# Keeping the seven x operands of six matrix products in DRAM after the first product, and GpSimd out of these products

## Chip, cores and metric

One NeuronCore of a Trainium2 chip runs the whole kernel. The metric is device time in microseconds (us) of one execution, as the median of several runs. The engines are named as the profile names them: PE (TensorE matmul), PEld (TensorE weight load), DVE (VectorE), ACT (ScalarE), POOL (GpSimd) and SP (SyncE, which here issues every DMA).

## What is computed

One layer of a hybrid encoder, for 2048 prompt tokens and 64 sample tokens (2112 rows), model width 1024, all in float32:

```
xn = rms_norm(x)                    # 2112 x 1024
xa, za, q, k, v, zb, ga, gb = split(xn @ w_in)      # eight blocks of 1024 columns
ya = rglru(conv(xa)) * silu(za)
yb = diff_attn(rms(q), rms(k), v) * silu(zb)
y  = x + (sigmoid(ga) * (ya @ w_proj_a) + sigmoid(gb) * (yb @ w_proj_b)) @ w_out
```

The case is about the products of `xn` with the six column blocks q, k, v, zb, ga and gb. They are run as six groups of 1024 x 1024 weights: v, then half of q with half of k, zb, the other halves of q and k, ga, gb.

## The kernel before

The kernel has four stages in time. The first makes xn, the products for xa and za and the recurrence ("Hawk" stage, 0 to about 490 us), and writes xn to the DRAM tile `xn_d`. The second, `Stage "a"` (490 to 1650 us), runs the six groups above. The third is the attention (to about 2554 us). The fourth, `Stage "d"`, runs three more groups with the same code: ya @ w_proj_a, yb @ w_proj_b and the output projection.

A group multiplies 2112 x 1024 by 1024 x 1024. It does one level of a Strassen-Winograd scheme: token tiles i and i + 8 (128 tokens each) and the two halves of the inner and of the output dimension are the 2 x 2 blocks of one **item**, and an item needs seven products in place of eight. The seven operands of x are the blocks A11, A12, A22 and the sums S1, S2, S3, S4; those of the weights are B11, T1, T2, B21, T3, B22, T4. Every operand is a float32 tile of 128 x 512 (x) or 128 x 2048 (w), and is split in a high and a low part (`hi` by a cast to fp32r on ACT, `lo` as the rest), since a float32 product is made of three fp32r matmuls (hi*hi, hi*lo, lo*hi: lines 63, 64 and 65 of `mm3`). With four blocks of 128 along the inner half, one product is 12 matmuls of 512 columns. This is a **slot**. `ITEMS` gives the order: items 0 and 1 take turns (14 slots), then items 2 and 3 alone (7 slots each), the 64 sample tokens "s" (5 slots, `sample`), items 4 and 5 alone, items 6 and 7 in turns: 61 slots in a group.

The order of the work is written by hand: `at(s, fn)` puts `fn` on the list of slot s, and `tick()` issues the list behind the product of that slot, weights (`plan_w`) ahead of x (`plan_x`). PE, DVE, ACT and POOL issue in exactly this order; the order of SP's queue is set by the framework's scheduler. Each engine works its queue in order, and an instruction that waits holds all behind it.

`plan_x` (line 162) for an item whose first slot is b: at b - 9 and b - 8 four loads of 256 KB from `xn_d` into raw tiles (`load`, line 169); at b - 6 to b - 4 the four sums (`add`, line 173: S1 and S2 on DVE, S3 and S4 on POOL); then for the operand of slot k at k - 4 its `hi` (line 178, ACT) and at k - 3 its `lo` (line 181: A11, S1, S3, S4 on POOL, the other three on DVE). Operands lie in `xo`, five buffers of two parts each, which a slot's products release.

`plan_w` (line 118) loads a group's weights (line 129) from b - 13 on, where b is the group's first slot, makes T1 to T4 (line 135, DVE) at b - 7, b - 5 and b - 1, and cuts the seven operands in high and low parts from b - 6 to b + 6. An operand is cut in two halves of 128 x 1024: two casts on ACT (line 143), then the low part of one half on DVE and of the other on POOL (line 145).

Results leave PSUM by ACT copies and DVE adds in `pair` (lines 222 to 247). In the q and k groups `out_qk` then squares (774), reduces (775), takes a root (787, 788, newton 55 to 57) and scales (797) every half on ACT and DVE; `turn_qk` transposes it on PE (812) into one of two PSUM buffers, and ACT, DVE (828 for q) and POOL (823, the low part of k) make its parts, of which two (q) or three (k) are stored, 256 KB each, in rows of 512 bytes (816). The other groups store a half once, after an ACT sigmoid for the gates (747, stored in 749), and after a DVE product too for zb (752, 753).

Of the kernel before, what the change touches and what calls it, by code (L numbers as in the profile page):

```python
# [11 lines left out]
F32 = mybir.dt.float32  # L12
# [7 lines left out]
P = 128  # L20
# [57 lines left out]
class Stage:  # L78
    def __init__(self, nc, tc, c, name, ident, order, bufs, first=()):
        self.nc, self.ident = nc, ident  # L80
        self.tc, self.c, self.first = tc, c, first
        pool = lambda n, b, **kw: c.enter_context(tc.tile_pool(name=n + name, bufs=b, reuse_waits=RW, **kw))
        place = lambda i: pool(f"wq{i}_", 1, side="right")
        self.wq = [place(i) for i in range(7)]
        self.xr = pool("xr", 2, side="right")
        self.xo = pool("xo", 5, side="right")
        self.wq += [place(i) for i in range(7, 15)]
        self.wfree = list(order)
        self.bufs = bufs
        self.sb = pool("sb", 1)  # L90
        self.wk = pool("wk", 1) if name == "a" else None
        self.pm = pool("pm", 4, space=PSUM)
        self.pz = pool("pz", 2, space=PSUM)
        self.pt = pool("pt", 2, space=PSUM)
        self.now = -99
        self.tasks = {}

    def at(self, s, fn):
        self.tasks.setdefault(max(s, self.now), []).append(fn)
# [23 lines left out]
    def plan_w(self, src, ws, b, pick):  # L123
        nc, q, at = self.nc, {}, self.at

        def load(nm, i):
            q[nm] = self.wtile(pick=pick)
            for k in range(0, 4, 2):
                nc.sync.dma_start(q[nm][1][:, k : k + 2, :], src[i, :, k : k + 2, :])

        def sub(dst, x, y, over=None):
            q[dst] = q[over] if over else self.wtile(pick=pick)
            for i in range(2):
                s = slice(2 * i, 2 * i + 2)
                nc.vector.tensor_tensor(q[dst][1][:, s, :], q[x][1][:, s, :], q[y][1][:, s, :], op=ALU.subtract)  # L135

        def cut(nm):
            at_, raw = q[nm]
            soon = pick if pick is None else nm in ("B11", "T1")
            (hi_at, hi), (lo_at, lo) = self.wtile(F32R, soon), self.wtile(F32R, soon)  # L140
            for i in range(2):
                s = slice(2 * i, 2 * i + 2)
                nc.scalar.copy(hi[:, s, :], raw[:, s, :])  # L143
                eng = nc.vector if i == 0 else nc.gpsimd
                eng.tensor_tensor(lo[:, s, :], raw[:, s, :], hi.bitcast(F32)[:, s, :], op=ALU.subtract)  # L145
            ws[nm] = hi, lo, (hi_at, lo_at)
            if nm != "T2":
                self.wfree.append(at_)

        at(b - 13, lambda: (load("B11", 0), load("B12", 1)))  # L150
        at(b - 8, lambda: load("B22", 3))
        at(b - 7, lambda: sub("T1", "B12", "B11"))
        at(b - 6, lambda: cut("B11"))
        at(b - 5, lambda: sub("T2", "B22", "T1"))
        at(b - 4, lambda: (load("B21", 2), cut("T1")))
        at(b - 2, lambda: cut("T2"))
        at(b - 1, lambda: (sub("T3", "B22", "B12", "B12"), sub("T4", "B21", "T2", "T2")))
        for i, nm in enumerate(("B21", "T3", "B22", "T4")):
            at(b + 2 * i, lambda nm=nm: cut(nm))


    def plan_x(self, src, item, xs, s, b):
        nc, q, at = self.nc, {}, self.at
        V, G = nc.vector, nc.gpsimd

        def load(nm, t, half):
            tn = TOK[t][1]
            q[nm] = self.raw(nm)
            nc.sync.dma_start(q[nm][:, :, :tn], src[t, :, half * 4 : half * 4 + 4, :tn])

        def add(eng, dst, x, y, op, over=None):
            q[dst] = q[over] if over else self.raw(dst)
            eng.tensor_tensor(q[dst], q[x], q[y], op=op)

        def hi(nm):
            o = self.xo.tile([P, 2, 4, P], F32R, name="x8")
            xs[nm] = o[:, 0], o[:, 1]
            nc.scalar.copy(xs[nm][0], q[nm])  # L178

        def lo(nm, eng):  # L180
            eng.tensor_tensor(xs[nm][1], q[nm], xs[nm][0].bitcast(F32), op=ALU.subtract)  # L181

        if item == "s":
            def both():
                o = self.xo.tile([P, 2, 4, P], F32R, name="x8")
                for i in range(2):
                    r = q[f"A{i}"][:, :, :TS]
                    xs[f"A{i}"] = o[:, i]
                    nc.scalar.copy(o[:, i, :, :TS], r)
                    V.tensor_tensor(o[:, i, :, TS:], r, o.bitcast(F32)[:, i, :, :TS], op=ALU.subtract)  # L190

            at(b - 5, lambda: (load("A0", NT - 1, 0), load("A1", NT - 1, 1)))
            at(b - 2, both)
            return
        u, v = item, item + 8
        at(b - 9, lambda: (load("A21", v, 0), load("A22", v, 1)))
        at(b - 8, lambda: (load("A11", u, 0), load("A12", u, 1)))
        at(b - 6, lambda: add(V, "S1", "A21", "A22", ALU.add))
        at(b - 5, lambda: (add(V, "S2", "S1", "A11", ALU.subtract), add(G, "S3", "A11", "A21", ALU.subtract, "A21")))
        at(b - 4, lambda: add(G, "S4", "A12", "S2", ALU.subtract))  # L200
        off = b - s[0]
        for nm, k, eng in zip(("A11", "S1", "S2", "A12", "S3", "S4", "A22"), s, (G, G, V, V, G, G, V)):
            at(k + off - 4, lambda nm=nm: hi(nm))
            at(k + off - 3, lambda nm=nm, eng=eng: lo(nm, eng))

# [77 lines left out]
        self.tick()  # L283


    def run(self, groups):
        plan, b = [], 0
        for g, (wsrc, xsrc, out) in enumerate(groups):
            ws = {}
            last = g == len(groups) - 1 and self.first  # L290
            self.plan_w(wsrc, ws, b, False if last else None)
            for its in ITEMS:
                n = len(its)
                gens = []
                for k, it in enumerate(its):
                    xs = {}
                    s = [b + i for i in range(5)] if it == "s" else [b + n * i + k for i in range(7)]
                    self.plan_x(xsrc, it, xs, s, s[0] - 1 if it == 4 else s[0])
                    gens.append((it, xs, ws, out, s))
                plan.append((gens, b))  # L300
                b += 5 if its == "s" else 7 * n
        self.now = -20
        while self.now < 0:
            self.tick() if self.now in self.tasks else self.skip()
        E = mybir.EngineType
        self.c.enter_context(self.tc.manual_schedule(engines={E.PE, E.DVE, E.Activation, E.Pool}))
        for items, b in plan:
            assert self.now == b
            gens = []
            for it, xs, ws, out, s in items:  # L310
                done = out(it, s)
                if it == "s":
                    self.sample(xs, ws, done)
                else:
                    gens.append(self.pair(it, xs, ws, done))
            for _ in range(7 if gens else 0):
                for g in gens:
                    next(g)
                    self.tick()
        while self.tasks:  # L320
            self.tick() if self.now in self.tasks else self.skip()
# [6 lines left out]
def stream_step_kernel(ctx, tc, I, O):  # L328
# [9 lines left out]
    m1_d = dram.tile([NT, P, D], F32, name="m1_d")  # L338
    strip_d = dram.tile([NH, P * STRIP], F32, name="strip_d")
    xn_d = dram.tile([NT, P, KT, P], F32, name="xn_d")  # L340
    ya_d = dram.tile([NT, P, KT, P], F32, name="ya_d")
    yb_d = dram.tile([NT, P, KT, P], F32, name="yb_d")
    mt_d = dram.tile([NT, P, KT, P], F32, name="mt_d")
# [382 lines left out]
    with ExitStack() as c:  # L726
# [81 lines left out]
        def turn_qk(h0, isk, t, c):  # L808
# [10 lines left out]
            if isk:  # L819
                kf, lo = new(), new()  # L820
                nc.scalar.mul(kf, pq, gk)
                nc.scalar.copy(hi.bitcast(F32R), kf)
                nc.gpsimd.tensor_tensor(lo.bitcast(F32R), kf, hi, op=ALU.subtract)
                put(kT_d, kf)
            else:
                nc.scalar.mul(hi.bitcast(F32R), pq, gq)
                lo = new()
                nc.vector.scalar_tensor_tensor(lo.bitcast(F32R), pq, gq, hi, op0=ALU.mult, op1=ALU.subtract)
# [3 lines left out]
        def strips():  # L832
# [25 lines left out]
            (I["wg"][2], xn_d, out_qk(4)),  # L858
            (I["wg"][4], xn_d, out_gate(ga_d, False)),
            (I["wg"][5], xn_d, out_gate(gb_d, False)),  # L860
        ])

    with ExitStack() as c:
        c.enter_context(tc.manual_schedule(engines={mybir.EngineType.PE}))
# [353 lines left out]
        def take(name):  # L1218
            slot = [9e9]
            rings[name][1].append(slot)  # L1220
            return slot
# [331 lines left out]
```

## Time and profile before

| | us |
|---|---|
| median of 3 runs (lowest to highest) | 3129.71 (3129.59 to 3131.15) |
| the profiled execution | 3132.76 |
| its span, first to last instruction | 3131.0 |
| PE busy in the span | 2854.5 (91%) |
| DVE busy | 2070.2 (66%) |
| ACT busy | 1703.7 (54%) |
| POOL busy | 1447.7 (46%) |
| DMA, share of 16 engines | 42.3%, 406.18 MB |

Busy time of PE counts matmuls that overlap, so it does not show how near PE is to its best; the distance from one matmul's start to the next does. A granted clock of 1.0 is TensorE's upper level, 0.5 its lower one.

### The profile page before, as it was taken

The numbers are of one execution on the slowest core, as the hardware profiler recorded it, in microseconds if no ns is written. First come the engines' busy times: TensorE is split into PE (matmuls) and PEld (weight loads), VectorE is DVE, ScalarE is ACT, GpSimd is POOL, SyncE is SP. The second block draws the span as 40 slices with busy tenths as digits, with TensorE's granted clock in tenths as the row PEclk, the third lists the DMA queues.
The fourth block names the chain that finished last, engine by engine and source line by source line (L and its number), as shares of the span: only waits on it lengthen the run. The fifth ranks groups of instructions, "written<-read, shape, count | busy, mean of one in ns | idle before, by whom it ended". The sixth has DMA issues, their size and how long they took to land.

```text
span 3131.0 us, 43652 instructions
## 1 busy us (share of the span) xinstructions
PE 2854.5 (91%) x14808; PEld 2392.7 (76%) x14808; DVE 2070.2 (66%) x4147; ACT 1703.7 (54%) x3251; POOL 1447.7 (46%) x900
## 2 busy tenths in 40 slices
PE   6999996999979989699997998998999979979899
PEld 6888885777758777587785987887888768868677
DVE  7776786267685776735525677777777775475764
ACT  7776774345544455545445766676676653333432
POOL 0000005355454544545544655555465457786743
PEclk9999998999989999899998999999999989989999
DMA  4121232335534346354346453544543434545553
GB/s 139 60 75 53 70 122 84 124 128 149 181 100 156 129 131 184 108 165 138 107 117 170 124 141 112 144 127 122 135 117 116 128 101 148 196 149 196 177 172 129
DMA packets 356671, 408.96 MB, mean 131 GB/s; under 512 B 48448, under 2 KB 242400, under 8 KB 356448
## 3 DMA queue, kind: packets, MB, share of 16 engines
q1 hardware_dynamic: 356448, 406.18, 42.3%
q8 instruction: 117, 1.92, 0.3%
q14 instruction: 106, 0.87, 0.1%
HBM read 272.22 MB, written 131.37 MB: 129 GB/s over the span
## 4 chain that ended last, share of the span: by engine, by line
PE 45%; DVE 11%; ACT 4%; issue 2%; POOL 2%; DMA 1%; SPq 0%; DVEq 0%; POOLq 0%; ACTq 0%
PE acc L65 7%; PE acc L63 7%; PE acc L64 7%; PE accv L1008 5%; PE pk L942 3%; PE pk L943 3%; PE ptt L1000 3%; PE accv L1131 2%; PE acz L65 1%; PE acz L63 1%; PE acz L64 1%; DVE o L1172 1%; DVE S L955 1%; ACT S L973 1%; DVE w L135 1%
## 5 line engine op out<-in xcount | busy, mean ns | idle before, releaser
L65 PE MATMUL acc<-w,x 128*128 128x512 f32 x1728 | 694.9, 402 | 82.8 <-POOL x L181 55.4
L63 PE MATMUL acc<-w,x 128*128 128x512 f32 x1728 | 699.0, 405 | 14.8 <-ACT sc L230 7.7
L64 PE MATMUL acc<-w,x 128*128 128x512 f32 x1728 | 689.0, 399 | 11.2 <-DVE w L145 10.8
L65 PEld LDWEIGHTS acc<-w,x 128*128 128x128 f32 x1728 | 334.8, 194 | 168.6 <-POOL x L181 64.1
L145 POOL TENSOR_TENSOR w<-w,w 128x1024 fp32r<-128x1024 f32 x63 | 180.1, 2860 | 574.7 <-ACT w L143 549.4
L63 PEld LDWEIGHTS acc<-w,x 128*128 128x128 f32 x1728 | 335.7, 194 | 87.1 <-ACT sc L230 8.5
L64 PEld LDWEIGHTS acc<-w,x 128*128 128x128 f32 x1728 | 335.2, 194 | 81.8 <-DVE w L145 11.8
L181 POOL TENSOR_TENSOR x<-xA,x 128x512 fp32r<-128x512 f32 x144 | 217.3, 1509 | 311.9 <-ACT x L178 298.2
L942 PE MATMUL pk<-k,Q 128*128 128x512 f32 (+2 forms) x640 | 263.2, 413 | 48.8 <-DVE S L955 17.7
L955 DVE TENSOR_SCALAR_CACHE_REDUCE S<-pk,far 128x1024 f32<-128x1024 f32 x224 | 226.2, 1014 | 118.5 <-PE pk L943 105.3
L1008 PE MATMUL accv<-v,tw 128*128 128x128 f32 x2176 | 295.7, 279 | 2.6 <-ACT o L1020 2.3
L1008 PEld LDWEIGHTS accv<-v,tw 128*128 128x128 f32 x2176 | 271.8, 195 | 9.2 <-ACT o L1020 4.2
L1001 ACT COPY tw<-ptt 128x512 f32<-128x512 f32 (+1 forms) x288 | 157.5, 556 | 150.3 <-PE ptt L1000 148.6
L973 ACT ACTIVATE S<-S,nm 128x1920 f32<-128x1920 f32 (+7 forms) x128 | 208.7, 1631 | 52.7 <-DVE nm L972 52.4
L64 PE MATMUL accb<-x,wh 128*128 128x384 f32 (+3 forms) x656 | 232.9, 355 | 2.9 <-DVE x L515 2.9
L181 POOL TENSOR_TENSOR x<-xS,x 128x512 fp32r<-128x512 f32 x144 | 209.9, 1462 | 54.0 <-ACT x L178 52.1
L63 PE MATMUL accb<-x,wh 128*128 128x384 f32 (+3 forms) x656 | 234.4, 357 | 0.2 <-ACT x L514 0.2
L981 POOL TENSOR_TENSOR S<-S,S 128x2048 f32<-128x2048 f32 (+3 forms) x64 | 232.5, 3633 | 4.4
L65 PE MATMUL accb<-x,wl 128*128 128x384 f32 (+3 forms) x656 | 232.8, 355 | 0.0
L943 PE MATMUL pk<-k,Q 128*128 128x512 f32 (+2 forms) x640 | 231.6, 368 | 0.0
L181 DVE TENSOR_TENSOR x<-xA,x 128x512 fp32r<-128x512 f32 x144 | 145.8, 1012 | 122.9 <-ACT x L178 122.9
L178 ACT CAST x<-xA 128x512 fp32r<-128x512 f32 x288 | 177.3, 621 | 75.0 <-PE acc L65 38.2
(253 smaller groups left out, 6152.9 us busy)
## 6 DMA issues: line engine op xcount, KB each, us to landing
xA<-xn_d SPq DMA_DIRECT2D x192, 256.0 KB, 3.0
w<-in_wg SPq DMA_DIRECT2D x72, 512.0 KB, 5.7
raw<-in_ckT SPq DMA_DIRECT2D x32, 512.0 KB, 4.2
Q<-qh_d SPq DMA_DIRECT2D x128, 128.0 KB, 2.8
Q<-ql_d SPq DMA_DIRECT2D x128, 128.0 KB, 2.9
raw<-in_cv SPq DMA_DIRECT2D x32, 512.0 KB, 3.9
raw<-in_w1b SPq DMA_DIRECT2D x32, 256.0 KB, 3.1
ya_d<-SZ SPq DMA_DIRECT2D x16, 512.0 KB, 3.3
```

Of the source, the lines that this page charges most:

```text
L63: nc.tensor.matmul(out, shi, mhi, start=start, stop=False, **kw)
L64: nc.tensor.matmul(out, shi, mlo, start=False, stop=False, **kw)
L65: nc.tensor.matmul(out, slo, mhi, start=False, stop=stop, **kw)
L145: eng.tensor_tensor(lo[:, s, :], raw[:, s, :], hi.bitcast(F32)[:, s, :], op=ALU.subtract)
L178: nc.scalar.copy(xs[nm][0], q[nm])
L181: eng.tensor_tensor(xs[nm][1], q[nm], xs[nm][0].bitcast(F32), op=ALU.subtract)
L942: nc.tensor.matmul(pk[:, o], Q[0][:, m, qs], kk, start=True, stop=False)
L943: nc.tensor.matmul(pk[:, o], Q[1][:, m, qs], kk, start=False, stop=True)
L955: nc.vector.tensor_scalar(s[:, k0 : k0 + f], pk[:, :f], far[:, h : h + 1], None, op0=ALU.add, op1=ALU.max, accum_out=mp[:, cx["j"] : cx["j ...
L973: nc.scalar.activation(s[:, :n], s[:, :n], AF.Exp, bias=nm, accum_out=sc[m])
L981: nc.gpsimd.tensor_tensor(S[0][:, :n], S[0][:, :n], S[1][:, :n], op=ALU.add)
L1008: nc.tensor.matmul(acc[:, r, :], tw[:, j, :], hd[kt // 8][1][:, kt % 8, :], start=kt == r == 0, stop=kt == 2 * p + 1)
```

## The change

In `Stage "a"` the first group makes the operands of x as before, with every sum and every low part on DVE, and stores each operand's high and low part to a new DRAM tile `xc_d` (57 operands of 128 x 2 x 512 floats: 56 of the items and one of the sample tokens; 256 KB for each part). The five later groups call `take` in place of all of `plan_x`: four slots ahead of its product an operand's two parts are loaded into the buffer of `xo`. Both halves of a weight's low part are made on DVE in this stage, and the low part of k as well. `Stage "d"` keeps its code: there `keep` is None, and `alone` is false.

```
-                eng = nc.vector if i == 0 else nc.gpsimd
+                eng = nc.vector if i == 0 or self.alone else nc.gpsimd
                 eng.tensor_tensor(lo[:, s, :], raw[:, s, :], hi.bitcast(F32)[:, s, :], op=ALU.subtract)
...
-    def plan_x(self, src, item, xs, s, b):
+    def plan_x(self, src, item, xs, s, b, keep=None, kept=None):
...
+        if kept is not None:
+            def take(k, nms):
+                o = self.xo.tile([P, 2, 4, P], F32R, name="x8")
+                for i in range(2):
+                    nc.sync.dma_start(o[:, i].bitcast(F32), kept[k, :, i])
...
+            if item == "s":
+                at(s[0] - 4, lambda: take(56, ("A0", "A1")))
+            for j, nm in enumerate(names if item != "s" else ()):
+                at(s[j] - 4, lambda j=j, nm=nm: take(7 * item + j, (nm,)))
+            return
+        V, G = nc.vector, nc.vector if keep is not None else nc.gpsimd
...
         def lo(nm, eng):
             eng.tensor_tensor(xs[nm][1], q[nm], xs[nm][0].bitcast(F32), op=ALU.subtract)
+            if keep is not None:
+                for i in range(2):
+                    nc.sync.dma_start(keep[7 * item + names.index(nm), :, i], xs[nm][i].bitcast(F32))
...
-                    self.plan_x(xsrc, it, xs, s, s[0] - 1 if it == 4 else s[0])
+                    self.plan_x(xsrc, it, xs, s, s[0] - 1 if it == 4 else s[0],
+                                keep if g == 0 else None, keep if g > 0 else None)
...
+    xc_d = dram.tile([57, P, 2, 4, P], F32, name="xc_d")
...
-                nc.gpsimd.tensor_tensor(lo.bitcast(F32R), kf, hi, op=ALU.subtract)
+                nc.vector.tensor_tensor(lo.bitcast(F32R), kf, hi, op=ALU.subtract)
```

## Rows read from the trace of the kernel before

**Rows 1.** Windows, the six groups: us, busy PE, PEld, DVE, ACT, POOL, PEclk, DMA, GB/s
```profile
490.00:686.00 196.00, 175.03 (x730) 136.33 (x730) 86.82 (x92) 76.89 (x123) 86.86 (x53) 0.95 0.37 120
686.00:884.00 198.00, 184.65 (x818) 148.86 (x817) 147.12 (x216) 100.67 (x182) 107.85 (x68) 0.94 0.51 154
884.00:1084.00 200.00, 175.19 (x747) 141.54 (x746) 130.65 (x153) 96.75 (x165) 97.02 (x61) 0.93 0.40 131
1084.00:1283.00 199.00, 181.81 (x818) 146.44 (x817) 147.28 (x219) 103.30 (x186) 105.03 (x67) 0.96 0.51 154
1283.00:1481.00 198.00, 173.62 (x743) 139.98 (x742) 104.57 (x122) 96.34 (x164) 93.47 (x60) 0.93 0.41 132
1481.00:1650.00 169.00, 164.46 (x714) 133.25 (x712) 70.66 (x76) 77.50 (x133) 78.70 (x56) 0.99 0.38 121
```
**Rows 2.** Waits of PE, 500 to 1650 us: us in total, times, longest
```profile
PE acc L65 <- POOL x L181: 43.3, 9, 18.1
PE ptx L812 <- DVE sf L828: 23.7, 5, 8.7
PE acc L65 <- DVE x L181: 22.0, 9, 4.3
PE acc L63 <- ACT sc L230: 7.7, 2, 3.9
PE acz L65 <- DVE x L181: 5.0, 2, 2.5
```
**Rows 3.** Waits of PE in the last group alone, 1481 to 1650 us
```profile
PE acc L65 <- POOL x L181: 4.2, 2, 3.5
```
**Rows 4.** Timeline of PE inside the last group: start, us, instruction; first and thirteenth matmul
```profile
1559.74 0.39 PE L65 MATMUL acc<-w,x 128*128 128x512 f32 x1
...
1562.46 0.39 PE L65 MATMUL acc<-w,x 128*128 128x512 f32 x1
```
**Rows 5.** Timeline of DVE and POOL: a low part beside POOL, then one with POOL idle
```profile
920.47 2.86 DVE L181 TENSOR_TENSOR x<-xS,x 128x512 fp32r<-128x512 f32 x1
...
920.33 2.46 POOL L145 TENSOR_TENSOR w<-w,w 128x1024 fp32r<-128x1024 f32 x1 [5.63 <-ACT w L143]
...
1618.17 0.69 DVE L181 TENSOR_TENSOR x<-xS,x 128x512 fp32r<-128x512 f32 x1 [2.03 <-ACT x L178]
```
**Rows 6.** Lines 145 and 181, whole span: ns lowest/median/highest, first and last start
```profile
L145 DVE TENSOR_TENSOR w<-w,w x63: 1206/1722/3426, 456.0 to 2984.3; 128x1024 fp32r<-128x1024 f32 x63
...
L181 DVE TENSOR_TENSOR x<-xS,x x72: 672/691/2889, 522.0 to 3095.2; 128x512 fp32r<-128x512 f32 x72
```
**Rows 7.** Timeline of POOL at the start of the first group
```profile
509.75 5.69 POOL L145 TENSOR_TENSOR w<-w,w 128x1024 fp32r<-128x1024 f32 x2 [12.09 <-DMA ya_d<-SZ]
515.40 2.24 POOL L181 TENSOR_TENSOR x<-xS,x 128x512 fp32r<-128x512 f32 x1
```
**Rows 8.** Lines of DVE in the second group, 686 to 884 us: busy us, mean ns, idle before
```profile
L135 DVE TENSOR_TENSOR w<-w,w 128x1024 f32<-128x1024 f32 x8 | 18.4, 2342 | 0.0
L181 DVE TENSOR_TENSOR x<-xA,x 128x512 fp32r<-128x512 f32 x16 | 14.8, 926 | 0.0
L145 DVE TENSOR_TENSOR w<-w,w 128x1024 fp32r<-128x1024 f32 x7 | 13.5, 1933 | 1.2 <-issue 0.9 <-ACT w L143 0.3
```
**Rows 9.** DMA, 700 to 860 us: GB/s in 40 slices of 4 us; queue: packets, MB, share
```profile
GB/s 2 0 70 131 67 264 44 116 0 168 219 176 131 140 263 310 211 66 118 262 262 211 71 193 228 330 233 1 8 123 4 35 191 255 252 214 173 374 279 234
...
q1 hardware_dynamic: 37503, 25.57, 53.0%
```
**Rows 10.** Tile xA, its loads: duration of an issue in ns, then us to landing
```profile
L169 SPq DMA_DIRECT2D xA<-xn_d x204: 319/327/908, 459.9 to 1597.8; - x102
...
DMA to landing us min/median/max: 2.3/3.1/7.7
```
**Rows 11.** Waits of SP's queue, 655 to 1650 us, and its timeline near 1089 us
```profile
SPq L749 <- ACT sc L747: 116.3, 47, 12.3
...
1089.50 14.98 SPq L753 DMA_DIRECT2D zb_d<-sf  x4
```

More of the change, by code (lines that the diff above doesn't have):

```diff
@@ L88, in __init__ @@
         self.wfree = list(order)
-        self.bufs = bufs
+        self.bufs, self.alone = bufs, name == "a"
         self.sb = pool("sb", 1)
@@ L159, in plan_w @@
             at(b + 2 * i, lambda nm=nm: cut(nm))
-    def plan_x(self, src, item, xs, s, b):
+    def plan_x(self, src, item, xs, s, b, keep=None, kept=None):
         nc, q, at = self.nc, {}, self.at
-        V, G = nc.vector, nc.gpsimd
+        names = ("A11", "S1", "S2", "A12", "S3", "S4", "A22")
+        if kept is not None:
[3 more added lines that the diff above has]
+                    nc.sync.dma_start(o[:, i].bitcast(F32), kept[k, :, i])
+                if len(nms) == 1:
+                    xs[nms[0]] = o[:, 0], o[:, 1]
+                else:
+                    xs.update({nm: o[:, i] for i, nm in enumerate(nms)})
+            if item == "s":
[4 more added lines that the diff above has]
+        V, G = nc.vector, nc.vector if keep is not None else nc.gpsimd
         def load(nm, t, half):
@@ L190, in both @@
                     V.tensor_tensor(o[:, i, :, TS:], r, o.bitcast(F32)[:, i, :, :TS], op=ALU.subtract)
+                    if keep is not None:
+                        nc.sync.dma_start(keep[56, :, i], o.bitcast(F32)[:, i])
             at(b - 5, lambda: (load("A0", NT - 1, 0), load("A1", NT - 1, 1)))
@@ L201, in plan_x @@
         off = b - s[0]
-        for nm, k, eng in zip(("A11", "S1", "S2", "A12", "S3", "S4", "A22"), s, (G, G, V, V, G, G, V)):
+        for nm, k, eng in zip(names, s, (G, G, V, V, G, G, V)):
             at(k + off - 4, lambda nm=nm: hi(nm))
@@ L283, in sample, with run @@
         self.tick()
-    def run(self, groups):
+    def run(self, groups, keep=None):
         plan, b = [], 0
@@ L860, in stream_step_kernel @@
             (I["wg"][5], xn_d, out_gate(gb_d, False)),
-        ])
+        ], xc_d)
     with ExitStack() as c:
```

## The prediction

> **What bounds the kernel now.** I read the windows first, one for each of the six groups that the change touches [rows 1]. The reader is to see that five groups take 196 to 200 us and the sixth 169 us, although all six have the same number of slots. Next the pace of PE: twelve matmuls, a slot, take 1562.46 - 1559.74 = 2.72 us when nothing holds it [rows 4], and a group's 712 matmuls (56 products of 12, 40 of the sample tokens) so take about 162 us. So the sixth group is close to PE's own pace, and the others lose some 30 us each. Then the waits of PE [rows 2]: the sum over the stage is 43.3 + 23.7 + 22.0 + 7.7 + 5.0 = 101.7 us, and three of the five rows, 70.3 us, end when a low part of x (line 181) is written, on POOL or DVE. The sixth group has 4.2 us of them [rows 3]. It alone has no next group whose weights are prepared beside its own work. So PE bounds the middle of a group, and the preparation by DVE, POOL and ACT bounds its edges, where weights and x are cut together.
>
> Why preparation is late there shows in the timeline: a low part of x takes DVE 0.69 us with POOL idle, and 2.86 us when it starts 0.14 us behind a POOL instruction of 2.46 us [rows 5]. The same spread stands in the extremes of both lines: 1206 to 3426 ns, and 672 to 2889 ns [rows 6]. POOL and DVE do not add up here; one waits while the other works.
>
> **The sum is made against** the profiled execution, 3132.76 us, which lies 3.05 us above the median; its span is 3131.0 us. I take 3 us off at the end.
>
> **Part 1, x out of groups two to six.** It removes per item four sums, seven casts and seven low parts. The waits on line 181 go with them: 70.3 us less the one of 18.1 us in the first group, about 52 us, less some 2 us of smaller ones in that group, which stay: 50 us. What is late next in the same places? The weights' low parts and, in the groups behind q and k, the DVE work on q and k. For that I count DVE in the second group: 147.1 us busy [rows 1]. 24 low parts and 17 sums leave, 41 x 0.926 = 38 us [rows 8]; seven weight halves of 1.21 us and 13 low parts of k of 0.69 us come from POOL [rows 6], 17 us. That is 126 us at today's slowed durations for about 180 us of group: DVE suffices on average. At the edge it does not quite: between the making of T1 and the last cut of T4 lie 14 slots, 38 us, and in them DVE has 8 + 14 instructions of 1.21 us for the weights, 26.6 us, and the q and k work of two items. The latter is (147.1 - 38 - 18.4 - 13.5) / 8.25 = 9.4 us for an item, 1.1 us more with the low part of k, so 21 us for two: 47.6 us in 38 us. So PE's waits on line 828, 23.7 us [rows 2], will not all go. I take half of the two rows that are not line 181 (23.7 + 7.7 = 31.4 us, and about 3 us of smaller waits): 17 us; the bounds are nothing and 34 us.
>
> **Part 2, the clock.** The granted clock is 0.93 to 0.96 in the first five groups and 0.99 in the sixth [rows 1]; twice the missing share of each window is its time at the lower level, in all 2 x (0.05 x 196 + 0.06 x 198 + 0.07 x 200 + 0.04 x 199 + 0.07 x 198 + 0.01 x 169) = 118 us. Work at the lower level takes twice as long, so the loss is half of what of this is not waiting: 8 us if all 101.7 us of waits lie in it, 59 us if none does. A second bound: with the sixth group without its waits, 165 us, as the unit, the other five hold 991 - 825 = 166 us more, and 97 us of that are waits; the 69 us left also hold the transposes of q and k and the strips' matmuls, which the sixth group lacks. I put the loss at 30 us, midway between 8 and 59. If two thirds of the waits go (50 + 17 of 102), so do two thirds of this, 19 us; bounds 8 and 28 us.
>
> **Part 3, the first group.** DVE takes over 4 of 7 low parts, two sums and half the cuts; two such instructions cost 0.69 and 1.21 us there in place of 2.24 and 2.85 us on POOL [rows 6, 7]. Steadily that is 22 x 0.69 + 6 x 0.7 = 19 us in 14 slots, covered by 38 us of PE. Its long wait of 18.1 us ends with the low part of S1, queued on POOL behind two weight halves of 5.69 us in all [rows 7]. After the change the same low part stands on DVE behind two halves of T2 and the sums T3 and T4, 6 x 1.21 = 7.3 us, instead of 5.69 + 2.24 us. I put it at nothing, with 8 us to either side. Its 114 stores go out from SP; a store waits for DVE's low part, and loads queued behind have nine slots of lead. That costs nothing unless SP falls behind by over 20 us.
>
> **Part 4, the loads.** Each of groups two to six loads 57 x 2 parts of 256 KB, 29.9 MB, in place of 8.7 MB. At today's mixture 25.57 MB take 53.0% of 160 us, 3.3 us for a MB, and the best 4 us slice moves 374 GB/s, 2.7 us for a MB [rows 9]. So 21.2 MB add 57 to 70 us of DMA time to a group. In q and k groups (now 0.51 x 198 = 101 us [rows 1]) this gives 158 to 171 us in some 180 us; in the others 121 to 150 us in 165 us. DMA stays under PE on average. What matters is lateness: a load may start when the product five slots back is done, four slots ahead of its own, 4 x 2.72 = 10.9 us. Two issues of 0.33 us and a landing of 3.1 us, at worst 7.7 us [rows 10], leave 7.1 us or 2.5 us. In front of a load may stand up to 2 MB of weights (5.4 us at the best rate) or the bursts of q and k stores, and SP itself: it has stood up to 12.3 us at a store that waited for ACT or DVE, and 15 us over four stores [rows 11]; today's loads have nine slots of lead and forgive this. Those waits come from the same late DVE and ACT and should shrink. I take 8 us of new waits in all five groups; bounds 0 and 45 us, the latter if each edge and each run of stores costs the 2 to 3 us by which the slack is short.
>
> Against this part speaks the Trainium skill, "DMA: Bandwidth & Descriptors", section "Anatomy of one DMA": about 2.0 us for each DMA plus bytes over 436 GB/s, so transfers of 256 KB would run at about 100 GB/s (estimate from that page). By it two loads would take 5.2 us of a 2.72 us slot, and the five groups would be some 700 us longer. The trace differs where the page is read as a rate: with transfers of the same size slices of 374 GB/s occur [rows 9], so the fixed part is a delay that overlaps, and I don't use it.
>
> **Sum:** -50 - 17 - 19 + 0 + 8 = -78 us; 3132.8 - 78 - 3 = 3052 us.
>
> **The rivals.**
> All waits of the edges go, those on line 828 too: -50 - 34 - 28 + 0 = -112 us, 3018 us. For it: DVE's 126 us are counted at slowed durations. Against: the 47.6 us in 38 us.
> The wait moves: DMA in the q and k groups, SP held by a late store, or DVE behind its own weights takes over, and 15 to 50 us of gain are left, 3080 to 3115 us. For it: 94% of DMA time at the upper count, and five buffers only. Against: the landings.
> Slower: the round trip from a buffer's release to both parts landed sets the pace. With five buffers a slot then takes (R + 2.72) / 5 us; it decides from R = 10.9 us. At R = 14 us a slot is 3.34 us, 0.62 us more, for 285 loads +177 us, less the 78 us: about 3230 us. For it: issue order on SP with waits of 12 us [rows 11]. Against: a landing of 7.7 us at worst [rows 10].
> No difference (within 6 us, 0.2%, about what a measurement of this kernel can tell from no change): needs new waits to equal the gain by accident.
> That the change does not do what it says I rule out: no call of these groups is left on POOL, and the fourth stage keeps its own path.
>
> **How the numbers follow.** Forecast 3052 us with its own range 3030 to 3080: 0.58. All gone: 0.13. The wait moves: 0.15. No difference: 0.04. Slower: 0.10. Faster is 0.58 + 0.13 + 0.15 = 0.86. The range takes in the first three but for the far ends of the second and third: 3010 to 3105 us.
>
> **What would show it.** In the profile after: no line 181 and no POOL in groups two to six; low parts of weights on DVE at 1.21 us, none at 3 us; groups two to five 165 to 185 us long each; a granted clock near 0.98; PE's waits on loads (a DMA into x) below 10 us in all. The first group should stay at 190 to 200 us. I am wrong if PE waits for loads in the middle of groups, if SP's stores hold loads for more than 7 us, or if line 828 keeps its 24 us.

## The result

The changed kernel takes 3024.99 us as the median of 3 runs (3022.78 to 3025.21), the kernel before 3129.71 us: a ratio of 0.9662 with a 95% interval of 0.9640 to 0.9684, 105 us less. The forecast was 3052 us, 78 us less, with a range of 3010 to 3105 us. The profiled execution is the median run itself, its span 3023.2 us.

The windows of the six groups after, in the columns of [rows 1]:

```profile
484.00:674.00 190.00, 171.60 (x727) 135.05 (x726) 101.16 (x142) 74.58 (x120) 0.00 (x0) 0.96 0.80 271
674.00:851.00 177.00, 175.47 (x820) 142.77 (x819) 108.51 (x203) 74.56 (x132) 0.00 (x0) 1.00 0.92 297
851.00:1028.00 177.00, 167.93 (x745) 136.92 (x744) 76.35 (x111) 63.34 (x101) 0.00 (x0) 0.97 0.79 266
1028.00:1204.00 176.00, 175.36 (x820) 142.62 (x819) 110.54 (x207) 76.16 (x134) 0.00 (x0) 1.00 0.92 297
1204.00:1381.00 177.00, 168.01 (x744) 137.22 (x743) 57.48 (x81) 64.19 (x102) 0.00 (x0) 0.97 0.81 269
1381.00:1543.00 162.00, 161.71 (x713) 132.35 (x711) 33.09 (x41) 47.86 (x78) 0.64 (x7) 1.00 0.76 244
```

The six groups take 1059 us in place of 1160 us. Groups two to five fall from 198 to 200 us to 176 or 177 us, the sixth from 169 to 162 us, the first from 196 to 190 us. The DMA share about doubles, POOL is gone, and in the second and fourth group the granted clock is 1.00 in the mean. The first stage ends some 6 us earlier too: PE starts the first group's first product at 483.8 us in place of 490.1 us.

PE's waits after, 485 to 1542 us, as [rows 2] has them for before:

```profile
PE acc L65 <- DVE x L197: 18.4, 1, 18.4
PE ptx L836 <- DVE sf L852: 17.1, 2, 9.0
PE acc L63 <- DMA x<-xc_d: 2.5, 3, 1.2
PE acc L63 <- ACT sc L251: 0.6, 2, 0.3
```

The five rows of before, 101.7 us (104.5 us with two small rows of the same view), have become 38.6 us. (Lines are counted anew: 197 is the old 181, 852 the old 828, 836 the old 812, 251 the old 230.) What remains is the first group's wait for S1's low part, two waits on the low part of q at the edges behind the q and k groups, and 2.5 us on the new loads.

DVE in the second group, beside [rows 8] (busy us, mean ns, idle before):

```profile
L821 DVE TENSOR_TENSOR sc<-sc,ya 128x512 f32<-128x512 f32 (+1 forms) x28 | 18.1, 687 | 0.5
L145 DVE TENSOR_TENSOR w<-w,w 128x1024 fp32r<-128x1024 f32 x14 | 16.5, 1220 | 5.4 <-ACT w L143 5.4
...
L135 DVE TENSOR_TENSOR w<-w,w 128x1024 f32<-128x1024 f32 x8 | 9.3, 1218 | 0.0
```

A weight instruction takes 1218 to 1220 ns in the mean, where it took 1933 and 2342 ns. Fourteen halves now cost DVE 16.5 us; seven cost it 13.5 us before.

The loads of x, as [rows 10] (landing is the time from a load's issue to its data's arrival), and then DMA from 690 to 840 us, as [rows 9]:

```profile
L169 SPq DMA_DIRECT2D x<-xc_d x570: 319/423/1882, 666.8 to 1529.5; - x190
...
DMA to landing us min/median/max: 2.5/4.3/8.8
```

```profile
q1 hardware_dynamic: 48094, 43.17, 91.0%
```

### The profile page after: what moved, and what is told of

The parts are those of the page before. It is cut to its first block, busy times and chain, and to the rows that moved or that the text cites. A ratio compares the mean times of both kernels' runs of the same rounds, so it can differ in the third digit from the quotient of the medians.

```text
span 3023.2 us, 43338 instructions
## 1 busy us (share of the span) xinstructions
PE 2815.6 (93%) x14808; PEld 2368.6 (78%) x14808; DVE 1865.0 (62%) x4061; ACT 1554.2 (51%) x2961; POOL 861.5 (28%) x536
## 4 chain that ended last, share of the span: by engine, by line
PE 70%; DVE 15%; ACT 8%; issue 3%; DMA 3%; POOL 1%; SPq 0%; ACTq 0%; DVEq 0%; POOLq 0%
PE acc L65 11%; PE acc L63 11%; PE acc L64 11%; PE accv L1032 6%; PE pk L966 3%; PE pk L967 3%; PE ptt L1024 3%; PE acz L65 2%; PE acz L63 2%; PE acz L64 2%; PE accv L1155 2%; PE accb L64 2%; PE accb L63 2%; PE accb L65 2%; DVE w L135 1%
## 5 line engine op out<-in xcount | busy, mean ns | idle before, releaser
L65 PE MATMUL acc<-w,x 128*128 128x512 f32 x1728 | 682.4, 395 | 36.5 <-DVE x L197 24.5
L63 PE MATMUL acc<-w,x 128*128 128x512 f32 x1728 | 689.2, 399 | 11.3 <-ACT w L143 8.2
L64 PE MATMUL acc<-w,x 128*128 128x512 f32 x1728 | 680.1, 394 | 12.0 <-DVE w L145 12.0
L65 PEld LDWEIGHTS acc<-w,x 128*128 128x128 f32 x1728 | 328.7, 190 | 113.1 <-DVE x L197 26.1
L63 PEld LDWEIGHTS acc<-w,x 128*128 128x128 f32 x1728 | 329.2, 191 | 83.4 <-ACT w L143 8.6
L64 PEld LDWEIGHTS acc<-w,x 128*128 128x128 f32 x1728 | 329.0, 190 | 80.1 <-DVE w L145 13.0
L255 DVE TENSOR_TENSOR sc<-sc,acz 128x512 f32<-128x512 f32 x72 | 49.4, 686 | 301.8 <-PE acz L65 293.2
L966 PEld LDWEIGHTS pk<-k,Q 128*128 128x128 f32 x640 | 123.9, 194 | 71.6 <-issue 23.2
L1004 POOL TENSOR_SCALAR S<-S,cf 128x2048 f32<-128x2048 f32 (+3 forms) x64 | 102.9, 1607 | 228.8 <-DVE cf L1003 91.4
L145 DVE TENSOR_TENSOR w<-w,w 128x1024 fp32r<-128x1024 f32 x105 | 139.2, 1357 | 45.4 <-ACT w L143 39.7
```

Source lines behind the costliest of these rows:

```text
L63: nc.tensor.matmul(out, shi, mhi, start=start, stop=False, **kw)
L64: nc.tensor.matmul(out, shi, mlo, start=False, stop=False, **kw)
L65: nc.tensor.matmul(out, slo, mhi, start=False, stop=stop, **kw)
L966: nc.tensor.matmul(pk[:, o], Q[0][:, m, qs], kk, start=True, stop=False)
L1004: nc.gpsimd.tensor_scalar(S[1][:, :n], S[1][:, :n], cf, 1.0, op0=ALU.mult, op1=ALU.mult)
```

## The experiments

Each kernel was run beside the kernel before on the same chip; ratios are to that kernel, and "us less" is worked out from the ratio. The changed kernel stands at 0.9662 (0.9640 to 0.9684).

**Two reasons for late preparation.** Theory A, the forecast's: at the edges DVE and POOL hold each other up, as [rows 5] show. Theory B: the amount of work on x is too much there. The first two kernels each make one half of the change alone.

POOL out, but x made in every group:

```
-                eng = nc.vector if i == 0 else nc.gpsimd
+                eng = nc.vector if i == 0 or self.alone else nc.gpsimd
-        V, G = nc.vector, nc.gpsimd
+        V, G = nc.vector, nc.vector if self.alone else nc.gpsimd
-                nc.gpsimd.tensor_tensor(lo.bitcast(F32R), kf, hi, op=ALU.subtract)
+                nc.vector.tensor_tensor(lo.bitcast(F32R), kf, hi, op=ALU.subtract)
```

> The kernel before, with all work of POOL in the six groups moved to DVE, and x still made in every group (no DRAM copies). Theory A, DVE and POOL held each other up: the instructions of 2 to 3 us at the edges fall to 0.69 and 1.21 us, and a good part of the 105 us comes without any load, about 3070 us. Theory B, the work on x itself was too much for the edges: DVE then has 47.6 + 22 x 0.69 = 63 us of work in the 38 us of an edge, waits stay or grow, 3115 to 3145 us.

Measured: 3076.25 us, ratio 0.9830 (0.9811 to 0.9849), 53 us less. Its waits of PE, 500 to 1590 us:

```profile
PE acc L65 <- DVE x L181: 52.0, 18, 18.4
PE ptx L812 <- DVE sf L828: 16.8, 6, 7.2
PE acc L63 <- ACT sc L230: 2.7, 2, 1.4
```

The trace is that of its slowest run, 3086.4 us. Its second group, beside [rows 1]:

```profile
676.00:863.00 187.00, 179.27 (x820) 144.77 (x818) 157.54 (x285) 101.27 (x183) 0.00 (x0) 0.98 0.54 162
```

Half of the gain comes with no transfer saved or added. In this group DVE does 69 instructions more than before, which at 0.68 us each are some 46 us of work, and is busy only 10 us longer (157.5 us after 147.1 us): its own instructions have become shorter, as theory A says. Without the first group's long one (18.1 and 18.4 us), the waits on line 181 fall from 52 to 34 us. Since 34 us stay, the work on x is also too much for the edges: both theories have a part. A third reason is not separated by any run: POOL is also slower at the same work (a low part of x takes it 1.26 us at the lowest, DVE 0.68 us), so what POOL made late would come earlier on DVE even if the two never met.

Loads in, but POOL where it was:

```
-                eng = nc.vector if i == 0 or self.alone else nc.gpsimd
+                eng = nc.vector if i == 0 else nc.gpsimd
-        V, G = nc.vector, nc.vector if keep is not None else nc.gpsimd
+        V, G = nc.vector, nc.gpsimd
-                nc.vector.tensor_tensor(lo.bitcast(F32R), kf, hi, op=ALU.subtract)
+                nc.gpsimd.tensor_tensor(lo.bitcast(F32R), kf, hi, op=ALU.subtract)
```

> The changed kernel with POOL kept where it was: half of the weights' low parts, the low part of k, and four low parts and two sums of x in the first group; x is loaded in groups two to six. Theory A (holding each other up): DVE's 22 weight instructions at an edge still meet seven of POOL's, waits on DVE lines of q and k and of weights stay, 3050 to 3070 us. Theory B (amount of work on x): x is gone, 3025 to 3035 us.

Measured: 3050.09 us, ratio 0.9742 (0.9725 to 0.9759), 81 us less; 24 us short of the changed kernel. Its longest waits of PE, 500 to 1565 us, and POOL and DVE at the edge behind the second group (start, us, instruction):

```profile
PE ptx L836 <- DVE sf L852: 21.8, 2, 11.6
PE acc L65 <- POOL x L197: 18.1, 1, 18.1
PE acc L63 <- DMA x<-xc_d: 6.1, 5, 2.4
...
869.47 2.55 POOL L145 TENSOR_TENSOR w<-w,w 128x1024 fp32r<-128x1024 f32 x1 [1.43 <-ACT w L143]
...
870.34 6.17 DVE L135 TENSOR_TENSOR w<-w,w 128x1024 f32<-128x1024 f32 x4
```

With x gone the waits on x go, and those on the low part of q stay about as they were in [rows 2]. The four sums of T3 and T4 take 6.17 us here, beginning under POOL's weight half, and 4.62 us in the changed kernel (shown with the run that makes T3 later). That is what A expects, and the time lies at the lower end of A's 3050 to 3070 us, not in B's 3025 to 3035 us. Not all of the 24 us is A's, though: PE's waits are 10.7 us longer than in the changed kernel, mainly 4.7 us on line 852 and 6.3 us on the loads (8.8 us in all rows; why these came later is open), and the first group begins some 5 us later. The two halves of the change together would be 53 + 81 = 134 us if they added; they give 105 us. That fits waits for a low part of x which either half removes: the first took 18 us of these 52 us, the second all.

**The first group.** Its x back on POOL, one line undone:

```
-        V, G = nc.vector, nc.vector if keep is not None else nc.gpsimd
+        V, G = nc.vector, nc.gpsimd
```

> The changed kernel with four low parts and two sums of x back on POOL in the first group alone. If the 6 us by which the first stage ends earlier and the 5.5 us of the first group come from POOL being out of DVE's way, they go: about 3035 us. If not, within 4 us of 3025 us.

Measured: 3030.38 us, ratio 0.9679 (0.9664 to 0.9693). The interval overlaps that of the changed kernel, so the time tells nothing. The trace tells half of it. PE's wait for the cast `ch` at the end of the first stage, in this run and then in the changed kernel:

```profile
PE pr L63 <- ACT ch L610: 7.1, 1, 7.1
...
PE pr L63 <- ACT ch L610: 2.5, 1, 2.5
```

It is 7.0 us in the kernel before and in the run with loads and POOL, the two others in which POOL prepares the first group's x, and 2.3 to 5.0 us in the runs in which it does not. The first group begins 5.9 us later than in the changed kernel (489.7 us), so POOL's work on the first group's x did reach into the stage before. The first group itself was no longer here: 188 us after 190 us. So the 6 us went, as the expectation said, and the 5.5 us of the first group did not.

**What still waits at the edges.** T3 made two slots later:

```
-        at(b - 1, lambda: (sub("T3", "B22", "B12", "B12"), sub("T4", "B21", "T2", "T2")))
+        at(b - 1, lambda: sub("T4", "B21", "T2", "T2"))
+        at(b + 1, lambda: sub("T3", "B22", "B12", "B12"))
```

> The changed kernel with the two sums of T3 moved from one slot before a group to the slot after its first (two slots later), nine groups. If the waits of 8.1 and 9.0 us on line 852 come from the burst of 4 x 1.22 us ahead of it in DVE's queue, each falls by at least 2.4 us and the first group's 18.4 us by 2.4 us too: 3010 to 3018 us. If DVE's whole backlog at the edge sets them, within 4 us of 3025 us.

The place in the changed kernel, DVE and then PE (start, us, instruction, idle before and its end):

```profile
856.51 0.68 DVE L799 TENSOR_REDUCE va<-sf 128x8 f32<-128x512 f32 x1
857.10 4.62 DVE L135 TENSOR_TENSOR w<-w,w 128x1024 f32<-128x1024 f32 x4
861.64 0.68 DVE L799 TENSOR_REDUCE va<-sf 128x8 f32<-128x512 f32 x1
862.24 2.35 DVE L145 TENSOR_TENSOR w<-w,w 128x1024 fp32r<-128x1024 f32 x2
864.50 0.75 DVE L852 SCALAR_TENSOR_TENSOR sf<-ptx,gq,sf 128x512 fp32r<-128x512 f32 x1
...
865.30 1.12 PE L836 MATMUL ptx<-ident,sc 128*128 128x128 f32 x4 [8.11 <-DVE sf L852]
```

Measured: 3021.64 us, ratio 0.9653 (0.9639 to 0.9668): not told apart from the changed kernel. Its trace shows the mechanism at a smaller size: the waits on the low part of q are 12.3 us in all in place of 17.1 us, so taking 2 x 1.22 us out of the burst did shorten each by about that much. The 18.4 us of the first group did not move: the queue in front of S1's low part there is 6.8 us long in both runs, so T3's sums were not what stood in it. Part of the gain was lost elsewhere: the wait for `ch` in the first stage is 5.0 us in place of 2.5 us, and in the fourth stage, where T3 also moved, the waits on weights' low parts are 13.9 us in place of 12.0 us.

**How much slack the loads have.** Lead of three slots, then of two:

```
-                at(s[0] - 4, lambda: take(56, ("A0", "A1")))
+                at(s[0] - 3, lambda: take(56, ("A0", "A1")))
-                at(s[j] - 4, lambda j=j, nm=nm: take(7 * item + j, (nm,)))
+                at(s[j] - 3, lambda j=j, nm=nm: take(7 * item + j, (nm,)))
```

> The changed kernel with each operand's two loads issued three slots ahead of its product instead of four: 3 x 2.72 = 8.2 us less two issues of 0.42 us leaves 7.3 us for a landing that takes 4.3 us in the middle and 8.8 us at most. If the lead is what keeps the loads off the path (theory A), only the slow landings show: up to 15 us of waits on loads, 3025 to 3040 us. If loads have slack to spare (theory B), 3025 us within 4.

> The same with two slots ahead: 5.4 us, less 0.84 us of issue 4.6 us for landings of 4.3 us in the middle. Theory A: about half of the 285 loads come late by 1 us or more, 150 to 350 us of waits on loads, 3150 to 3350 us. Theory B: under 3040 us.

Measured: 3038.24 us with three slots, ratio 0.9700 (0.9680 to 0.9719), and 3049.51 us with two, in one run. With two slots PE waits for loads as follows (485 to 1565 us; the changed kernel has 2.5 us):

```profile
PE acc L63 <- DMA x<-xc_d: 13.4, 7, 4.0
PE acc L65 <- DMA x<-xc_d: 5.4, 4, 2.1
```

The lead matters, as theory A said. With three slots the time lies in its 3025 to 3040 us, though the interval still touches that of the changed kernel (0.9680 against 0.9684); the waits on loads are 8.3 us, and the q and k groups 183 and 181 us long in place of 177 and 176 us. For two slots A's 3150 to 3350 us were far too much, and B's limit of 3040 us was passed too. The expectation took half of the 285 loads as late, with 4.6 us of time for landings of 4.3 us in the middle. There were eleven waits in all, ten of them in the q and k groups, where the stores of q and k share the queue, and only these groups became clearly longer (189 us each; groups three and five 177 and 178 us).

**How near DMA is to its limit.** A third transfer of 256 KB, DRAM to DRAM, behind each operand's two:

```
                     nc.sync.dma_start(o[:, i].bitcast(F32), kept[k, :, i])
+                self.nj += 1
+                nc.sync.dma_start(self.junk[self.nj], kept[k, :, 0])
```

> The changed kernel with a third transfer behind each operand's two, 256 KB from DRAM to DRAM, which nothing reads: 57 x 0.262 = 15 MB more for each of five groups. If the DMA engines are as near their limit as their share says (0.92 of 177 us in q and k groups, 0.76 to 0.81 in the others), 15 MB at 2.7 to 3.1 us for a MB are 40 to 46 us: 203 to 209 us of DMA time in a q and k group, 175 to 190 us in the others, so about 27 to 32 us more for two groups and 0 to 20 us for three: 3080 to 3150 us. If the share overstates (packets wait on each other and are counted as busy), under 3045 us.

Measured: 3071.28 us, in one run. Its windows for groups two to five:

```profile
674.00:862.00 188.00, 179.09 (x816) 144.01 (x815) 108.45 (x203) 74.65 (x132) 0.00 (x0) 0.98 1.02 334
862.00:1042.00 180.00, 168.74 (x746) 136.78 (x744) 78.36 (x114) 64.39 (x102) 0.00 (x0) 0.98 0.96 329
1042.00:1241.00 199.00, 184.68 (x816) 144.43 (x817) 109.02 (x204) 75.87 (x133) 0.00 (x0) 0.97 1.01 335
1241.00:1421.00 180.00, 169.42 (x746) 136.76 (x745) 59.63 (x83) 64.27 (x102) 0.14 (x1) 0.98 0.96 337
```

The q and k groups saturate, with a DMA share of 1.02 and 1.01 at 334 GB/s, and become 11 and 23 us longer; the others take 180 us in place of 177 us. The time lies between the two ranges, 3080 to 3150 us and under 3045 us. DMA binds in the q and k groups here, so a share of 0.92 at 297 GB/s was near the limit: with transfers in plenty four groups move 329 to 337 GB/s. How near, the share does not say exactly, as 0.96 goes with 337 GB/s and 1.02 with 334 GB/s. The 27 to 32 us for a q and k group were too much. The third issue of each operand on SP is not told apart from its bytes.

**The fourth stage.** The same without POOL in its preparation:

```
-                eng = nc.vector if i == 0 or self.alone else nc.gpsimd
+                eng = nc.vector
-        V, G = nc.vector, nc.vector if keep is not None else nc.gpsimd
+        V = G = nc.vector
```

> The changed kernel with POOL's part of the preparation of weights and x moved to DVE in the fourth stage too (three groups, x made there as before; POOL keeps one product for each result half). If holding each other up costs there what it cost in the six groups (10 us a group in the run without POOL and without loads), 2995 to 3010 us. If DVE's amount of work at the edges binds there, 3020 to 3040 us.

Measured: 2998.31 us, ratio 0.9571 (0.9554 to 0.9588), faster than both kernels. The three groups of this stage, the changed kernel first, then this one:

```profile
2446.00:2641.00 195.00, 172.68 (x723) 138.00 (x724) 109.33 (x119) 69.43 (x115) 137.06 (x87) 0.92 0.49 161
2641.00:2843.00 202.00, 183.77 (x830) 147.50 (x830) 133.96 (x114) 79.31 (x136) 148.35 (x91) 0.96 0.57 185
2843.00:3019.00 176.00, 168.25 (x732) 135.83 (x731) 105.38 (x111) 59.07 (x102) 88.42 (x53) 0.98 0.47 151
```

```profile
2443.00:2625.00 182.00, 170.17 (x724) 136.86 (x725) 129.84 (x172) 69.94 (x116) 50.25 (x31) 0.95 0.56 176
2625.00:2816.00 191.00, 181.25 (x828) 145.49 (x827) 144.98 (x171) 78.95 (x136) 61.52 (x34) 0.97 0.58 190
2816.00:2990.00 174.00, 168.77 (x736) 136.44 (x733) 111.61 (x162) 59.05 (x102) 6.10 (x4) 0.98 0.47 154
```

POOL gives up 87 us of busy time in the first of them and DVE gains only 21 us for 53 instructions more, some 36 us of work at 0.68 us each. The time lies in theory A's range, in a place that the change had not touched; that POOL is slower at the same work has its part here too.

**Together.** Without POOL in the fourth stage's preparation as well, with T3 later in the six groups alone, and then with x issued ahead of the weights in the first group besides:

```
+        at(b + 1 if self.alone else b - 1, lambda: sub("T3", "B22", "B12", "B12"))
+        at(b - 1, lambda: sub("T4", "B21", "T2", "T2"))
...
-            self.plan_w(wsrc, ws, b, False if last else None)
+            if g or not self.alone:
+                self.plan_w(wsrc, ws, b, False if last else None)
...
+            if g == 0 and self.alone:
+                self.plan_w(wsrc, ws, b0, False if last else None)
```

> No POOL in the fourth stage's preparation either, as in the run before, and T3 made two slots later in the six groups alone. If the two gains (27 us, and 3 to 4 us in the six groups) add: 2993 to 2997 us. If the later T3 gains nothing by itself: 2998 us within 4.

> The same, and in the first of the six groups x is issued ahead of the weights in each slot's list. If the 18.4 us that PE waits for the low part of S1 are its place in the queues of ACT and DVE behind T2's cuts, PE goes on two slots further before it needs T2: the wait falls by 4 to 6 us, 2988 to 2992 us. If the recurrence's last work on ACT and DVE (to 499.7 us in the changed kernel) holds all of them, the wait moves to another operand and the time stays within 3 us of the run beside it.

Measured: 2998.16 us, ratio 0.9572 (0.9558 to 0.9586), and 2993.43 us, ratio 0.9563 (0.9547 to 0.9579). Neither is told apart from the run without POOL in the fourth stage, so the later T3 gains nothing that the time shows. In the last one the 18.4 us become a wait of 8.9 us for a weight's low part and one of 5.5 us for x, and the first group is 187 us long in place of 191 us: the order did hold PE, and behind it the weights' low parts start as late as ever, 19.6 us behind the group's first product (part 3 below).

## Why the prediction was right, and where it was off

**The bound and its place.** Right. All of the gain but the first stage's 6 us lies in the six groups (1160 to 1059 us), and in groups two to five mostly at their edges.

**Part 1, waits.** The step said -50 us on line 181 and -17 us on the others, with 8 us of new waits, -59 us in all; measured -63 us. The waits on line 181 in groups two to six went completely. Of the others, which were to lose half, line 828 lost 6.6 of 23.7 us and line 230 lost 7.1 of 7.7 us. The count of 47.6 us of DVE work at an edge holds: from the making of T1 to the last cut of T4 behind the second group DVE is busy 46.2 us. These slots, 38 us at PE's pace, took 53 us, and the fence on that edge shows the queue in front of line 852.

**Part 2, the clock: the term that was mis-sized.** It was put at 19 us, with bounds of 8 and 28 us. The six groups lost 101 us, 63 us of it waits; 38 us are left for the clock and the restarts. Counted from the distances between matmul starts where PE did not wait, work at a slower pace took 47 us before and 15 us after, 32 us less. Twice the missing share of each window is now 2 x (0.04 x 190 + 0.03 x 177 + 0.03 x 177) = 36 us at the lower level, where it was 118 us: 82 us less, of which half, 41 us, is the most that it can give back (the shares are rounded, so both sums are rough). So most of the lower-clock time that went had been spent working, not waiting. The failing step is the loss of 30 us, midway between 8 and 59: it lay nearer the upper end. The two thirds of it held (82 of 118 us, beside 63 of 102 us of waits). The bounds do not follow from the step's own numbers: two thirds of 8 and 59 us are 5 and 39 us, not 8 and 28, and 38 us lies within them. Long waits left the clock low for the work behind them, and with no wait over 1.2 us in the second and fourth group it is at 1.00 there. That the waits drive it is argued; no run changed the clock by itself. The run with two slots of lead comes nearest: its q and k groups have 17.7 us more waits than in the changed kernel and are 26 us longer, at 0.98 in place of 1.00.

**Part 3, the first group.** Put at nothing, within 8 us; it gave 6 us, which are among the 101 us, and the stage before it another 6 us, which the prediction did not look for. Its long wait stayed (18.4 us after 18.1 us). The queue in front of S1's low part is as long as the step said, 6.8 us. But the step left out why this queue starts so late, although [rows 7] show it: POOL stood idle for 12.09 us until a store of the recurrence's result to `ya_d` had landed. After the change DVE waits for the same landing:

```profile
503.38 2.36 DVE L145 TENSOR_TENSOR w<-w,w 128x1024 fp32r<-128x1024 f32 x2 [3.43 <-DMA ya_d<-SZ]
...
510.20 1.28 DVE L197 TENSOR_TENSOR x<-xS,x 128x512 fp32r<-128x512 f32 x2
```

Both queues start 19.6 us behind the group's first product, so the wait is the store's first and the queue's second. The last experiment shows that the order of the queue was part of it.

**Part 4, the loads.** DMA time was put at 158 to 171 us in the q and k groups and 121 to 150 us in the others; the shares give 0.92 x 177 = 163 us and 0.76 x 162 = 123 us to 0.81 x 177 = 143 us. The new waits were 2.5 us, below the 8 us taken. The worst landing was 8.8 us, a little over the 7.7 us of before. The Trainium skill's "DMA: Bandwidth & Descriptors", section "Anatomy of one DMA", with 2.0 us for each DMA plus the bytes, fitted there to transfers that GpSimd issues, would have made this 700 us slower when read as a rate (an estimate). The trace disagrees with that reading: transfers that SP issues, most of them of 256 KB, ran at 297 GB/s through whole groups here and at 334 GB/s in the run with more of them.

**The rivals.** The time lies below the forecast's own range of 3030 to 3080 us, and inside the stated one only since that takes in a rival. This rival, "all waits go", was put at 3018 us and is nearer in time (7 us) than the forecast (27 us), but not in mechanism: line 852 kept 17.1 us. The 27 us are about 19 us more from the clock, 6 us from the first stage and 4 us more of waits, less the 3 us taken off at the end. "Slower", a round trip over 10.9 us, was far: even with 5.4 us of lead the kernel takes 3049.51 us. "The wait moves" did not happen, though the run with more transfers shows that DMA would be next in the q and k groups.

## What to carry to other kernels

An instruction of DVE whose mean is well above its lowest time, with POOL busy beside it, is a sign that giving POOL's work to DVE may make both finish earlier; count DVE's demand at the lowest times before judging that it has no room. Look at the edges between repeated blocks separately from their middles, and price a wait there together with the lower clock seen behind it. A load that replaces computation needs two counts: the share of DMA time in each stretch and the lead against its worst landing.

## What the runs showed of the hardware

DVE and POOL wait for each other for whole instructions: the low part of 2.86 us of [rows 5] ended at 923.33 us, 0.54 us behind the end of POOL's instruction at 922.79 us. In the run with loads and POOL a DVE instruction that takes 0.17 us elsewhere took 2.08 us and ended at 868.08 us, POOL's beside it at 868.05 us:

```profile
865.58 2.47 POOL L145 TENSOR_TENSOR w<-w,w 128x1024 fp32r<-128x1024 f32 x1 [10.95 <-ACT w L143]
...
866.00 2.08 DVE L55 SCALAR_TENSOR_TENSOR tmpa<-ya 128x16 f32<-128x16 f32 x1
```

POOL's low part of x, 1.26 us at the lowest, took 2.24 us in [rows 7], beside sums on DVE. The Trainium skill says so on "SBUF — State Buffer", section "SBUF: two separate sides": an instruction of VectorE with two SBUF inputs and one of GpSimd that reads SBUF take the shared port pair by turns, each for all of its length. The traces agree. What moving POOL's work to DVE was worth in this kernel the runs tell: 53 us of 3130 us in six groups, and some 27 us more in three. How much of that is the waiting for each other, and how much that DVE is faster at the same work, no run separates.

DMA engines at a share of 0.92, 297 GB/s with transfers mostly of 256 KB, delayed PE by only 2.5 us in five groups; at 1.02 the two q and k groups became 11 and 23 us longer.
